# One decoder layer on one core: when the weight splits around the first stick-breaking head are queued

## The chip, the cores and the metric

The kernel runs on one core of one Trainium2 chip. The metric is the device time of one execution in microseconds. The kernel before took 1089.22 us, the median of three runs (1088.9 to 1090.16). A change of less than about 0.2% (2.2 us) can hardly be told from no change here.

The engines are named as the profile names them: PE (TensorE, matrix products), PEld (its weight loads), DVE (VectorE), ACT (ScalarE), POOL (GpSimd) and SP (SyncE, whose queue issues most loads).

## What is computed

One layer of a decoder on 512 tokens of width 1024, all in fp32. A combined projection of the input gives queries, keys and values for three kinds of attention, and gates. The branch that matters here is stick-breaking attention, eight heads of 64 columns:

```python
z = jnp.einsum('bhqd,bhkd->bhqk', qi, kt).astype(jnp.float32) * scale
log_keep = jnp.where(before, jax.nn.log_sigmoid(-z), 0.0)
later = lax.cumsum(log_keep, axis=3, reverse=True) - log_keep
a = jnp.where(before, jnp.exp(jax.nn.log_sigmoid(z) + later), 0.0)
return jnp.einsum('bhqk,bhkd->bhqd', a.astype(vt.dtype), vt)
```

The other two branches (differential and dilated attention) follow in time, then the output projection, a layer norm, an MLP and a second layer norm. None of these is touched.

## The kernel before, in words

**Products in fp32 precision.** Every fp32 operand is written as a high part (rounded to the matrix format) and a low part (the rest), and a product is three matmuls: high by high, high by low, low by high. A weight block of 128x1024 arrives from DRAM as `raw`; the *split* of a block is one ACT cast (`wh<-raw`, L227) and one DVE subtraction (`wl<-raw,wh`, L228). It is issued by `split_next` through `issue_split`.

**Items and blocks.** The work is a list of items, in the order of the main loop (L1326). An item is a group of 24 matmuls into one PSUM bank, and its evacuation (`ev`) is issued at the start of the next turn of the loop. The items and weight blocks that matter here are these:

| turn n | item | blocks it needs |
|---|---|---|
| 0 | queries and keys of the first pair of heads (`sb_q 0`, `sb_k 0`), two banks | 0 to 12 (input and first weights) |
| 1, 2 | `sb_q 1`, `sb_k 1` | 13; 14 |
| 3 to 6 | the first 512-column group: values `sb_v`, four row tiles | 15 to 18, all four for each tile |
| 7 to 10 | `sb_q 2`, `sb_k 2`, `sb_q 3`, `sb_k 3` | 19; 20; 21; 22 |

The items use two PSUM banks (tag `mm`) in turn: item 3 needs the bank of item 1 evacuated, item 4 that of item 2. Item 1 is evacuated by `evac_twice` (ACT L125, L126, L129, L131; DVE L108 twice, L130, L132) and item 2 by `evac_stacked` (ACT L115, L116; DVE L108 twice).

**How far ahead blocks are split.** `pump(limit, most)` issues at most `most` splits, and no further than `limit + 7` blocks, for seven pairs of `wh`/`wl` buffers; `fill` issues the loads, four `raw` buffers deep, so that the load of a block follows the split of the block four before. Up to the loop, blocks 0 to 13 are split. Then one block is split in turn 0 and one in turn 1 (blocks 14 and 15), two in turn 2 (16, 17), two in turn 3 (18, 19), and one each in turns 4 and 5 (20, 21). The limit stops turn 6; block 22 follows in turn 7.

**The heads.** `step` (L1302) advances the attention heads, which are generators, in between. Head 0 starts in the middle of turn 1: its score matmuls (L138, L139, masks L1004 and L1007) and then its softplus in three parts, `bi` = 2, 1, 0. A part is Abs, Exp, Ln on ACT (L1015 to L1017), then max-and-add, cast and subtraction on DVE (L1018, L1021, L1022). Part 2 is issued in turn 1, part 1 in turn 2, part 0 in turn 3. Triangle matmuls (L1048, L1052) use the results.

**What sets the order on each engine.** Each engine works through its queue in order, but the queue is not the source order. A planner fills it: source order is the priority, and an instruction further down goes first when the planner reckons that the earlier one cannot start yet. In the trace of before, the cast of block 15 sits between L131 and L115 though the source has it behind both. `tc.issue_after(x)` forces what is issued inside it to stand behind `x` on `x`'s own engine. The list `tie` is used for that: head 0's part 2 puts its Ln (ACT) and its subtraction L1022 (DVE) into it, and `issue_split` then keeps the splits of turns 2 to 4 (blocks 16 to 20) behind them; `tie` is emptied in turn 4.

Of the kernel before, what the change touches and what calls it, by code (L numbers as in the profile page):

```python
# [12 lines left out]
AF = mybir.ActivationFunctionType  # L13
# [42 lines left out]
def trunk(tc, a, out):  # L56
    nc = tc.nc
    es = ExitStack()
    with es:
# [85 lines left out]
        st = {"dma": 0, "sum": 0, "split": 0}  # L145
# [61 lines left out]
        tie = []  # L207
# [7 lines left out]
        def split_next():  # L215
            c = chunks[st["split"]]
            w = c["w"]
            if c.get("dst") is None:
                h = ring.tile([P, 1024], F32R, name=nm("wh"), tag="wh", bufs=RING)
                lo = ring.tile([P, 1024], F32R, name=nm("wl"), tag="wl", bufs=RING)  # L220
                parts = [(h[:, :w], lo[:, :w], 0, w)]
                c["h"], c["l"] = parts[0][:2]
            else:
                parts = c["dst"]
            for h, lo, a0, a1 in parts:
                raw = c["from"]["raw"][:, a0:a1]
                nc.scalar.copy(h, raw)  # L227
                i = nc.vector.tensor_sub(lo, raw, h.bitcast(F32))  # L228
                st["low"] = getattr(i, "ins", i)
            c["from"]["uses"] -= 1  # L230
            st["split"] += 1
# [760 lines left out]
        def sb_head(hd):  # L992
            pr, side = hd // 2, hd % 2
            rs = (A, B)[side]
            while ("sb_q", pr) not in T or ("sb_k", pr) not in T:
                yield
            blk = [(0, 0, 0, 512), (1, 1, 0, 384), (2, 2, 0, 256), (3, 2, 256, 256)]
            bank = [at_bank() for _ in range(3)]
            for kb, bi, c0, n in reversed(blk):
                ps = bank[bi][:, c0:c0 + n]  # L1000
                mm_pair(ps, T["sb_k", pr], T["sb_q", pr], side, slice(kb * P, kb * P + P), slice(S - n, S),
                        kb != 2, False)
                if kb == 3:
                    nc.tensor.matmul(ps, identb, mask_b.rearrange("p a b -> p (a b)"), start=False, stop=False,  # L1004
                                     skip_group_check=True)
                else:
                    nc.tensor.matmul(ps[:, 0:P], identb, mask_b[:, 1, :], start=False, stop=False,  # L1007
                                     skip_group_check=True)
            w = [512, 384, 512]
            sph, spl, later = {}, {}, {}  # L1010
            for bi in (2, 1, 0):
                n = w[bi]
                ps = bank[bi][:, :n]
                e = slot("e")[:, :n]
                nc.scalar.activation(e, ps, AF.Abs)  # L1015
                nc.scalar.activation(e, e, AF.Exp, scale=-1.0)
                ln = nc.scalar.activation(e, e, AF.Ln, bias=1.0)  # L1017
                nc.vector.scalar_tensor_tensor(e, ps, 0.0, e, op0=OP.max, op1=OP.add)  # L1018
                h = slot("sph", F32R)[:, :n]
                lo = slot("spl", F32R)[:, :n]  # L1020
                nc.vector.tensor_copy(h, e)  # L1021
                low = nc.vector.tensor_sub(lo, e, h.bitcast(F32))  # L1022
                if hd == 0 and bi == 2:

                    tie[:] = [getattr(i, "ins", i) for i in (ln, low)]
                sph[bi], spl[bi] = h, lo

                if bi == 2:
                    later[2] = (256, (h[:, HC], lo[:, HC]))
                    sm = slot("sm")[:, HB]  # L1030
                    nc.vector.tensor_add(sm, e[:, HB], e[:, HC])
                    hl = slot("smp", F32R)
                    nc.vector.tensor_copy(hl[:, HB], sm)
                    nc.vector.tensor_sub(hl[:, HC], sm, hl[:, HB].bitcast(F32))
                    later[1] = (256, (hl[:, HB], hl[:, HC]))
                elif bi == 1:
                    nc.vector.tensor_add(e[:, 128:384], e[:, 128:384], sm)
                    h = slot("smh", F32R)[:, :n]
                    lo = slot("sml", F32R)[:, :n]
                    nc.vector.tensor_copy(h, e)  # L1040
                    nc.vector.tensor_sub(lo, e, h.bitcast(F32))
                    later[0] = (384, (h, lo))
                yield
            ah, al = {}, {}
            for kb, bi, c0, n in reversed(blk):
                ps = bank[bi][:, c0:c0 + n]
                for hl in (sph, spl):
                    nc.tensor.matmul(ps, tri_r, hl[bi][:, c0:c0 + n], start=False, stop=False, skip_group_check=True)  # L1048
                if kb < 3:
                    n2, hl = later[kb]  # L1050
                    for t in hl:
                        nc.tensor.matmul(bank[bi][:, c0 + n - n2:c0 + n], ones_r, t, start=False, stop=False,  # L1052
                                         skip_group_check=True)
                if kb == 3:
                    continue
                n = w[bi]
                e = slot("a")[:, :n]
                nc.scalar.activation(e, bank[bi][:, :n], AF.Exp)
                h = slot("ah", F32R)[:, :n]
                lo = slot("al", F32R)[:, :n]  # L1060
                nc.vector.tensor_copy(h, e)
                nc.vector.tensor_sub(lo, e, h.bitcast(F32))
                ah[bi], al[bi] = h, lo
                if kb != 1:
                    yield
            while ("sb_v", 0, 3) not in V:
                yield
            po = at_bank()
            for kb, bi, c0, n in blk:
                v = V["sb_v", 0, kb][hd // 4][:, hd % 4]  # L1070
                nc.tensor.matmul(po[:, S - n:S], v.rearrange("p two d -> p (two d)"), ah[bi][:, c0:c0 + n],
                                 start=kb == 0, stop=False, skip_group_check=True)
                nc.tensor.matmul(po[A, S - n:S], v[:, 0, :], al[bi][:, c0:c0 + n], start=False, stop=kb == 3,
                                 skip_group_check=True)
            done = 4 + pr in oT
            if not done:
                oT[4 + pr] = slot("oT")
            t = slot("ot")
            nc.scalar.copy(t[A], po[B, :])
            nc.vector.tensor_add(oT[4 + pr][rs, :], po[A, :], t[A])  # L1080
            if done:
                split_sb(pr)
            yield
# [240 lines left out]
        freed = 8  # L1324
        prev = None
        for n, it in enumerate(items):  # L1326
            if n == first_branch[0]:
                while any(4 + k not in oTs for k in range(8)):
                    step()
            if n == first_da[0]:  # L1330
                while active or waiting:
                    step()
            need = it["need"] or it["c"]
            while any("h" not in c for c in need):
                pump(freed, 1)
            if prev is not None:
                prev[0]["ev"](prev[1])

            pump(freed, 1 if n < 10 and n != 2 else 2)
            if n == 4:  # L1340
                tie.clear()
                with tc.issue_after(st["load"]):
                    load_consts()
            if n == 10:
                with tc.issue_after(st["low"]):
                    make_lam()
            if n == 13:
                pending.append(tables())
            if n == 22:
                turn_tables()  # L1350
            if n == DA_TABS:
                da_tables()
            if n == DA_TABS + 4:
                turn_da()
            if n == wout_at - 9:
                load_pT()
            if n == wout_at - 1:
                ln_consts("ln1_g", "ln1_b")
                for tt in range(4):
                    load_xn(tt)  # L1360
            if n == wout_at + 24:
                ln_consts("ln2_g", "ln2_b")
            if n > 1:
                step()
            ps = it["bank"]() if it["bank"] else mm_bank()
            for _ in it["mm"](ps) or ():
                if HALF:
                    step()
            freed += len(it["c"])
            pump(freed, 0 if n < 10 else 2)  # L1370
            prev = (it, ps)
            if n + 1 < len(items) and n >= wout_at and pending:
                pass
# [99 lines left out]
```

## Time and profile before

| | |
|---|---|
| median of three runs | 1089.22 us |
| profiled execution | 1088.82 us, span 1087.1 us |
| PE busy | 1074.0 us, 99% of the span |
| DVE busy | 691.8 us, 64% |
| ACT busy | 477.6 us, 44% |
| mean granted TensorE clock | 0.996 |

A row of the timeline gives start (us), duration (us), engine, line, operation, output and input, shape, count, and in square brackets the idle time of the engine before it with what ended it. A matmul row lasts longer than the step to the next one, since matmuls overlap: the pace is read from the starts. A row of the table by windows gives the stretch, its length, and for each engine its busy time and instructions, then the granted clock (1.00 is full), the busy share of the DMA engines and GB/s.

### The profile page before, as it was taken

Reading aid. Unit: us, or ns where it says so; the run is one execution under the profiler, and the core shown is the slowest. Engines: PE = TensorE matmul, PEld = TensorE weight load, DVE = VectorE, ACT = ScalarE, POOL = GpSimd, SP = SyncE. Lnnn points to the kernel's source line nnn. Section 1 sums busy time; section 2 is a strip of 40 time slices with the busy share of each in tenths; the row PEclk is TensorE's granted clock in tenths of the full one; section 3 lists DMA queues with packets and bytes.
Section 4 is the critical chain, followed back from the end, with each engine's and each line's share of the span. In section 5 each row is a group of like instructions: output and inputs, shape, how many; then the busy total and the mean of one; then the engine's idle time right before and its main releaser. Section 6 shows DMA issues by size and latency. Waiting matters only on the chain.

```text
span 1087.1 us, 13105 instructions
## 1 busy us (share of the span) xinstructions
PE 1074.0 (99%) x4991; PEld 894.2 (82%) x4991; DVE 691.8 (64%) x1245; ACT 477.6 (44%) x795; POOL 31.3 (3%) x55
## 2 busy tenths in 40 slices
PE   9899999999999999999999999999999999999997
PEld 6788788999888888888888888888888888888886
DVE  5788577657453757655444463866686686686676
ACT  6665445335232545454333232323554454454441
POOL 0000200000000000000000020110000000000000
PEclk9999999999999999999999999999999999999998
DMA  7432412031322113222233352253222422322402
GB/s 251 128 108 75 117 59 94 24 116 63 112 78 78 60 38 107 68 78 87 90 99 103 98 203 97 82 180 103 82 97 80 134 97 79 135 96 79 135 1 78
DMA packets 32431, 105.71 MB, mean 97 GB/s; under 512 B 4378, under 2 KB 5290, under 8 KB 32368
## 3 DMA queue, kind: packets, MB, share of 16 engines
q1 hardware_dynamic: 29424, 96.91, 27.4%
q0 software_dynamic: 2368, 7.05, 2.0%
q8 instruction: 39, 0.64, 0.2%
q10 hardware_dynamic: 576, 0.92, 0.2%
q14 instruction: 24, 0.20, 0.1%
HBM read 102.74 MB, written 2.12 MB: 96 GB/s over the span
## 4 chain that ended last, share of the span: by engine, by line
PE 94%; DVE 3%; DMA 1%; ACT 1%; issue 1%; DVEq 0%; SPq 0%
PE mm L87 17%; PE mm L89 17%; PE mm L88 17%; PE mm L337 3%; PE mm L339 3%; PE mm L338 3%; PE mm L679 2%; PE mm L681 2%; PE mm L680 2%; PE at L679 2%; PE at L681 2%; PE at L680 2%; PE mm L510 1%; PE mm L574 1%; PE mm L575 1%; PE mm L509 1%
## 5 line engine op out<-in xcount | busy, mean ns | idle before, releaser
L227 ACT CAST wh<-raw 128x1024 fp32r<-128x1024 f32 (+1 forms) x173 | 178.2, 1032 | 290.1 <-PE mm L88 222.8
L228 DVE TENSOR_TENSOR wl<-raw,wh 128x1024 fp32r<-128x1024 f32 (+1 forms) x173 | 206.1, 1196 | 104.6 <-ACT wh L227 100.6
L87 PE MATMUL mm<-xhT,wh 128*128 128x512 f32 x496 | 196.5, 396 | 0.0
L89 PE MATMUL mm<-xhT,wl 128*128 128x512 f32 x496 | 194.2, 391 | 0.1
L88 PE MATMUL mm<-xlT,wh 128*128 128x512 f32 x496 | 193.8, 391 | 0.0
L89 PEld LDWEIGHTS mm<-xhT,wl 128*128 128x128 f32 x496 | 93.1, 188 | 20.2 <-DVE wl L228 0.5
L87 PEld LDWEIGHTS mm<-xhT,wh 128*128 128x128 f32 x496 | 93.3, 188 | 19.5 <-issue 1.1
L88 PEld LDWEIGHTS mm<-xlT,wh 128*128 128x128 f32 x496 | 93.3, 188 | 17.8
L88 PE MATMUL mm<-x1lT,wh 128*128 128x512 f32 x256 | 99.6, 389 | 0.0
L89 PE MATMUL mm<-x1hT,wl 128*128 128x512 f32 x256 | 99.6, 389 | 0.0
L87 PE MATMUL mm<-x1hT,wh 128*128 128x512 f32 x256 | 99.6, 389 | 0.0
L337 PE MATMUL mm<-wh,xhT 128*128 128x512 f32 x160 | 65.5, 409 | 2.4 <-DVE sb_kb L108 2.3
L339 PE MATMUL mm<-wh,xlT 128*128 128x512 f32 x160 | 63.6, 398 | 0.0
L338 PE MATMUL mm<-wl,xhT 128*128 128x512 f32 x160 | 63.6, 397 | 0.0
L89 PEld LDWEIGHTS mm<-x1hT,wl 128*128 128x128 f32 x256 | 48.1, 188 | 10.1
L88 PEld LDWEIGHTS mm<-x1lT,wh 128*128 128x128 f32 x256 | 48.1, 188 | 10.0
L87 PEld LDWEIGHTS mm<-x1hT,wh 128*128 128x128 f32 x256 | 48.0, 188 | 9.9
L227 ACT CAST wh<-wsum 128x1024 fp32r<-128x1024 f32 x28 | 29.5, 1055 | 52.5 <-PE mm L88 49.3
L228 DVE TENSOR_TENSOR wl<-wsum,wh 128x1024 fp32r<-128x1024 f32 x28 | 34.2, 1222 | 24.2 <-ACT wh L227 23.6
L337 PEld LDWEIGHTS mm<-wh,xhT 128*128 128x128 f32 x160 | 38.2, 239 | 6.4 <-issue 2.7
L339 PEld LDWEIGHTS mm<-wh,xlT 128*128 128x128 f32 x160 | 38.3, 239 | 4.0
L338 PEld LDWEIGHTS mm<-wl,xhT 128*128 128x128 f32 x160 | 38.5, 241 | 3.5
(348 smaller groups left out, 1969.1 us busy)
## 6 DMA issues: line engine op xcount, KB each, us to landing
raw<-in_wt_dram SPq DMA_DIRECT2D x62, 512.0 KB, 3.4
raw<-in_wu_dram SPq DMA_DIRECT2D x32, 512.0 KB, 3.4
raw<-in_wd_dram SPq DMA_DIRECT2D x32, 512.0 KB, 3.3
raw<-in_wv_dram SPq DMA_DIRECT2D x20, 512.0 KB, 3.4
raw<-in_wb_dram SPq DMA_DIRECT2D x8, 512.0 KB, 3.3
raw<-in_wo_dram SPq DMA_DIRECT2D x8, 512.0 KB, 4.0
raw<-in_wg_dram SPq DMA_DIRECT2D x8, 512.0 KB, 3.9
rawx<-in_xT_dram SPq DMA_DIRECT2D x8, 256.0 KB, 5.1
```

Source lines behind the costliest of these rows:

```text
L87: nc.tensor.matmul(ps, wh, xh, start=start, stop=False, skip_group_check=True)
L88: nc.tensor.matmul(ps, wh, xl, start=False, stop=False, skip_group_check=True)
L89: nc.tensor.matmul(ps, wl, xh, start=False, stop=stop, skip_group_check=True)
L227: nc.scalar.copy(h, raw)
L228: i = nc.vector.tensor_sub(lo, raw, h.bitcast(F32))
L337: nc.tensor.matmul(ps, x1, c["h"][:, s], start=k == 0, stop=False)
L338: nc.tensor.matmul(ps, x1, c["l"][:, s], start=False, stop=False)
L339: nc.tensor.matmul(ps, x2, c["h"][:, s], start=False, stop=k == 7)
L509: nc.tensor.matmul(ps, h[:, q], c["l"][:, s], start=False, stop=False)
L679: nc.tensor.matmul(ps, h[:, q], c["h"][:, s], start=go, stop=False, skip_group_check=True)
L680: nc.tensor.matmul(ps, h[:, q], c["l"][:, s], start=False, stop=False, skip_group_check=True)
L681: nc.tensor.matmul(ps, lo[:, q], c["h"][:, s], start=False, stop=end, skip_group_check=True)
```

## The change

Three things are edited, all in the order of issue; no computation is added or removed.

1. The number of splits per turn: turn 1 issues three (blocks 15, 16, 17) where it issued one, turn 2 one (18) where it issued two, and turns 3 and 4 none where they issued two and one. Turns 5 to 9 then issue blocks 19 to 23, one each. The source comes back to the old count at turn 11.
2. Blocks 16 and 17 are issued ahead of head 0's first softplus part and are not tied. Instead that part's Abs is forced to stand behind the last cast issued so far on ACT, which is that of block 17.
3. Every softplus part of head 0 now rewrites `tie`, and `tie` is emptied in turn 8. So block 18 (turn 2) is tied behind part 2, and blocks 19 to 22 (turns 5 to 8) are tied behind part 0's Ln on ACT and its subtraction on DVE. Block 23 (turn 9) is not tied.

The small constants (`load_consts`) are still issued in turn 4 behind the last load issued by then.

```diff
@@ split_next
-                nc.scalar.copy(h, raw)
+                i = nc.scalar.copy(h, raw)
+                st["cast"] = getattr(i, "ins", i)
@@ sb_head
-                nc.scalar.activation(e, ps, AF.Abs)
+                with ExitStack() as behind:
+                    if hd == 0 and bi == 2:
+
+                        behind.enter_context(tc.issue_after(st["cast"]))
+                    nc.scalar.activation(e, ps, AF.Abs)
...
-                if hd == 0 and bi == 2:
+                if hd == 0:
 
                     tie[:] = [getattr(i, "ins", i) for i in (ln, low)]
@@ main loop
-            pump(freed, 1 if n < 10 and n != 2 else 2)
+            pump(freed, {1: 3, 3: 0, 4: 0}.get(n, 1 if n < 10 else 2))
+            if n == 8:
+                tie.clear()
             if n == 4:
-                tie.clear()
                 with tc.issue_after(st["load"]):
                     load_consts()
```

## The prediction

> **What bounds the kernel now.** The list of what PE waited for comes first, since PE is busy 99% of the span. Columns: who waited, for whom, us in total, times, the longest.
>
> ```profile
> PE mm L337 <- DVE sb_kb L108: 2.3, 1, 2.3
> PE at L845 <- DVE rel L881: 1.3, 1, 1.3
> PE at L1048 <- DVE spl L1022: 0.9, 1, 0.9
> PE at L318 <- ACT wh L227: 0.4, 1, 0.4
> ```
>
> These four are all the waits of matmuls in the whole run. The second and fourth belong to the start. The other two are one place, and the table by windows shows what follows them:
>
> ```profile
> 40.00:44.00 4.00, 0.98 (x4) 0.81 (x5) 3.84 (x8) 0.86 (x2) 0.00 (x0) 0.97 0.90 259
> 44.00:48.00 4.00, 4.00 (x12) 3.11 (x12) 3.26 (x7) 0.87 (x2) 0.00 (x0) 0.60 0.41 139
> 48.00:54.00 6.00, 6.00 (x28) 4.95 (x27) 0.85 (x2) 2.43 (x6) 0.00 (x0) 1.00 0.00 0
> ```
>
> Between 40 and 44 us PE is busy for 0.98 us and DVE for 3.84: for these few us DVE is the bound. After it PE is busy again, but at a granted clock of 0.60. The timeline of PE gives the size of the loss:
>
> ```profile
> 35.18 0.39 PE L339 MATMUL mm<-wh,xlT 128*128 128x512 f32 x1
> ...
> 39.26 0.40 PE L339 MATMUL mm<-wh,xlT 128*128 128x512 f32 x1
> 39.50 0.33 PE L1048 MATMUL at<-sph,tri_r 128*128 128x384 f32 x1
> 40.74 0.44 PE L1048 MATMUL at<-spl,tri_r 128*128 128x384 f32 x1 [0.92 <-DVE spl L1022]
> 41.02 0.39 PE L1052 MATMUL at<-smp,ones_r 128*128 128x256 f32 x2
> 43.69 0.71 PE L337 MATMUL mm<-wh,xhT 128*128 128x512 f32 x1 [2.27 <-DVE sb_kb L108]
> ...
> 47.18 0.40 PE L339 MATMUL mm<-wh,xlT 128*128 128x512 f32 x1
> 47.41 0.40 PE L337 MATMUL mm<-wh,xhT 128*128 128x512 f32 x1
> ...
> 62.54 0.39 PE L87 MATMUL mm<-xhT,wh 128*128 128x512 f32 x1
> ...
> 75.70 0.34 PE L1048 MATMUL at<-sph,tri_r 128*128 128x384 f32 x1
> ...
> 76.29 0.40 PE L1048 MATMUL at<-sph,tri_r 128*128 128x512 f32 x1
> ```
>
> From 35.18 to 39.26 PE does 18 steps, 0.227 us each. From 39.50 to 47.41 it does two L1048, two L1052 and nine item matmuls (8 at half pace, for 43.69 to 47.18 is 3.49 us where 8 x 0.227 = 1.81 would do). Undisturbed, the first four take 76.29 - 75.70 = 0.59 us (the same four for head 1, between the last two rows) and the nine 2.04, together 2.63. The stretch took 7.91, so **5.3 us** are lost here: 0.92 + 2.27 of waiting, 1.7 by the clock, and 0.4 in hand-overs. That is 0.48% of the time, and the most that this region can give back. As no matmul waits later, what is gained here reaches the end.
>
> Why DVE is late, from its timeline (first rows of the region to the release of PE):
>
> ```profile
> 24.50 0.69 DVE L108 SCALAR_TENSOR_TENSOR sb_kb<-at,sb_kb 64x512 fp32r<-64x512 f32 x1
> 27.46 0.69 DVE L1018 SCALAR_TENSOR_TENSOR e<-at,e 128x512 f32<-128x512 f32 x1 [2.26 <-ACT e L1017]
> 28.18 0.43 DVE L1021 CAST sph<-e 128x512 fp32r<-128x512 f32 x1
> 28.64 0.69 DVE L1022 TENSOR_TENSOR spl<-e,sph 128x512 fp32r<-128x512 f32 x1
> ...
> 29.59 1.22 DVE L228 TENSOR_TENSOR wl<-raw,wh 128x1024 fp32r<-128x1024 f32 x1
> ...
> 30.93 1.22 DVE L228 TENSOR_TENSOR wl<-raw,wh 128x1024 fp32r<-128x1024 f32 x1
> ...
> 33.10 0.69 DVE L108 SCALAR_TENSOR_TENSOR sb_qlb<-mm,sb_qb 64x512 fp32r<-64x512 f32 x1
> ...
> 34.74 2.36 DVE L228 TENSOR_TENSOR wl<-raw,wh 128x1024 fp32r<-128x1024 f32 x2
> ...
> 37.60 1.21 DVE L228 TENSOR_TENSOR wl<-raw,wh 128x1024 fp32r<-128x1024 f32 x1
> ...
> 39.00 1.22 DVE L228 TENSOR_TENSOR wl<-raw,wh 128x1024 fp32r<-128x1024 f32 x1
> ...
> 42.85 0.69 DVE L108 SCALAR_TENSOR_TENSOR sb_kb<-mm,sb_kb 64x512 fp32r<-64x512 f32 x1
> ...
> 46.23 0.42 DVE L350 TENSOR_TENSOR sb_v<-mm,sb_v 128x256 fp32r<-128x256 f32 x1 [0.44 <-ACT sb_v L349]
> ```
>
> DVE idles 2.26 us at 25.2, then works without a pause until item 2's keys are evacuated at 43.54. The six subtractions in between are blocks 16 to 21, of which 19 to 21 are for items 7 to 9; item 7's first matmul is the L87 row at 62.54.
>
> **The change, part by part.**
>
> *Blocks 16 and 17 ahead of the first softplus.* Two casts and two subtractions move, no instruction is added. On ACT they meet this:
>
> ```profile
> 20.84 1.05 ACT L227 CAST wh<-raw 128x1024 fp32r<-128x1024 f32 x1
> 21.92 0.59 ACT L115 ACTIVATE sb_ka<-at 64x512 fp32r<-64x512 f32 x1
> 22.52 0.59 ACT L116 ACTIVATE sb_kb<-at 64x512 fp32r<-64x512 f32 x1
> 25.50 0.60 ACT L1015 ACTIVATE e<-at 128x512 f32<-128x512 f32 x1 [2.38 <-PE at L1007]
> ...
> 36.50 1.06 ACT L227 CAST wh<-raw 128x1024 fp32r<-128x1024 f32 x1 [0.59 <-DMA raw<-in_wt_dram]
> 37.46 0.59 ACT L115 ACTIVATE sb_ka<-mm 64x512 fp32r<-64x512 f32 x1
> ```
>
> The casts take 2 x 1.05 = 2.10 of ACT's 2.38 idle us (23.1 to 25.2), so Abs still starts at 25.5: cost 0, covered by the wait for the score matmuls; without that cover it is 2.1. On DVE the subtractions take 2 x 1.22 = 2.44 from 25.19, so L1018 starts at 27.63 and not 27.46: 0.17 us. Their old places fall free, 2.44 us ahead of 43.54.
>
> *The wait of Abs behind the cast of block 17.* Behind the cast stand Abs and all of the softplus, whose DVE steps and L1048 wait for it. It costs something only if block 17's data come late. The loads of that group issued after 18 us (durations of the issue in ns) and all landing times from 18 to 24 us are these:
>
> ```profile
> DMA to landing us min/median/max: 3.4/3.4/4.2
> L185 SPq DMA_DIRECT2D raw<-in_wv_dram x2: 328/328/328, 18.6 to 20.3; - x2
> ```
>
> Block 17 is the first: 18.6 + 4.2 = 22.8 at the latest, ahead of 24.15 where its cast would start. Bounds 0 and 0.6 (ACT's wait for a load at 36.50); I take 0, since the load is in by 1.3 us. On SP load 19 still follows the split of 15; loads 20 and 21 follow 16 and 17, whose subtractions end near 26.4 and 27.6 and not at 30.8 and 32.2, so they come some 4 us earlier. Load 23 follows split 19 and comes later, for a block of item 11. The seven small constants now stand in SP's queue behind load 22 and ahead of 23; their readers come at turn 10 and after. Cost 0.
>
> *Blocks 19 to 21 behind part 0.* Three subtractions, 3.66 us, and three casts leave the stretch ahead of 43.54. Their new cover is behind part 0: in the 48 to 54 row DVE idles for 5.15 of 6 us and ACT for 3.57, room for four subtractions (4.88) and three casts (3.15), ahead of item 7, which on the new time scale starts at 62.54 - 5.3 = 57.2. On DVE the rows up to the L350 at 46.23 leave no room before. Without that cover each late block costs PE its lateness. Bounds: 0, and 5.3 if the first one is done only when item 7 starts in before; I take 0, since the idle row is next to part 0's end. Head 1's softplus, which shares these engines, can be put off by at most the same three splits, and its triangle matmuls with it; PE has items 5 and 6 to do meanwhile.
>
> *Blocks 22 and 23.* 22 waits for the buffer pair that item 6 frees, before and after. 23 is issued in turn 9 and not 8, two items ahead of its use: 2 x 24 x 0.227 = 10.9 us of matmuls cover a split of 2.3. Cost 0; without the cover 2.3.
>
> *The sum.* DVE would reach 43.54 + 0.17 - 2.44 - 3.66 = 37.6 with item 2's evacuation. If part 0's three DVE steps (0.69 + 0.43 + 0.69 = 1.81) come forward into the space, 39.4. ACT permits it: 37.46, where L115 stands, loses casts 16, 17, 20, 21 and the wait, 4 x 1.05 + 0.59 = 4.8 us. PE, freed of the 0.92 as L1022 is earlier by the same 6 us, asks for the bank at 39.50 + 0.59 = 40.1. Next late is item 3's evacuation for item 5, asked for at 40.1 + 24 x 0.227 = 45.5. It ended at 46.23 + 0.42 = 46.65, and with 16 and 17 gone from in front of it at 44.4 even if 19 to 21 stay there. So both waits go, and with them the half clock: -5.3. I give back 0.3 for hand-overs: -5.0. From the profiled 1088.82 (span 1087.1 + 1.72 around it) that gives 1083.8; the median is 0.4 above the profiled run, so **1084.2**.
>
> **The clock rule.** Here 2.27 us of waiting, 0.92 before, and 0.4 to 0.98 us of work between led to 3.5 us at half pace. The Trainium skill, "TensorE: Matmul & The Clock Gate", section "What's actually happening", states that the clock falls after an idle window of some 3.4 us and comes back after a busy one, the windows running free. The length of the slow stretch agrees (3.49); the wait that led to it is shorter than the rule's, 2.27, or 3.19 with both. By the rule a leftover wait of 1 or 2 us would cost no clock (a leftover of 2 gives -3.3), by the row it may cost 1.7 again (-1.6).
>
> **Rivals.**
>
> *A. The wait moves to the other bank.* Item 3 needs item 1's evacuation, and PE now fills the time until then with head 1's scores:
>
> ```profile
> 31.92 0.28 PE L138 MATMUL at<-sb_qb,sb_kb 128*128 128x256 f32 x1
> ```
>
> The evacuation ends with the L108 at 33.10, at 33.8. If the planner puts item 3 ahead of these scores, PE stands from 31.9. One of the two subtractions ahead of that L108 goes, so it ends at 33.8 - 1.22 + 0.17 = 32.7: wait 0.8; at 33.8 if other work fills in: 1.9. With or without 1.7 of clock the gain is 1.7 to 4.5, 1084.7 to 1087.5, middle 1086.1. For it: DVE is full there. Against: the planner's order avoids this wait now.
>
> *B. The casts go ahead of the first keys.* Block 15's cast stands ahead of L115 (20.84), so 16 and 17 could too. Then sb_ka waits 2 x 1.22 = 2.4 us more on DVE, the scores with it; PE waits up to 2.4, plus 1.7 of clock, while DVE's idle time comes back. The old waits still go, for 3.66 us leave DVE and 3.2 are needed. Gain 1.2 to 5.3; I put it at 1086.3 to 1088.0, the half of full price, since item 2 could fill the wait.
>
> *C. It does nothing.* Part 0 and the head's sums take all the space freed on DVE, and item 2's keys stay late: 1089.2. From 37.6 it takes 2.5 us of other work ahead of L108 before PE waits at all and 5.9 to restore the old wait; part 0 has 1.81. Hardly.
>
> *D. Slower: a starved item 7.* Split 19 now stands behind part 0 and has the lowest priority of what is in the queue by then. This is where the subtraction of block 25 stands now:
>
> ```profile
> 64.32 1.21 DVE L228 TENSOR_TENSOR wl<-raw,wh 128x1024 fp32r<-128x1024 f32 x1
> ```
>
> If the planner puts block 19's there, it ends at 65.5; PE waits 65.5 - 57.2 = 8.3 us, plus 1.7 of clock: -5.3 + 10.0 = +4.7, 1093.9. It decides from an end at 63 on (57.2 + 5.8, with 5.8 + 1.7 - 5.3 = 2.2). Against it: the idle engines from 48 to 54, and no other reader of these engines that is more urgent there.
>
> **How the numbers follow.** Forecast 0.50, A 0.17, B 0.13, C 0.06, D 0.14 (with whatever else the new order delays). Forecast and A are faster by over 0.2% (under 1087.0; that bound is about what a measurement tells from no change), and half of B: 0.735. Within it lie the other half of B and C: 0.125. Slower: D. Forecast, A and B hold 0.80, so the range reaches from 1083.3 (the full 5.3 and 0.6 of scatter, as the runs before have) to 1088.0, B's end. The likeliest case alone: 1083.3 to 1085.4 (a rest of 1.2 us).
>
> **What would show it.** Right: two subtractions between sb_kb and L1018 in DVE's timeline with no idle 2.26; Abs still near 25.5; at most one subtraction of a block between L1022 of part 2 and sb_kb of item 2; no row of PE with sb_kb or spl as releaser; granted clock 1.00 from 40 to 48; item 7's first L87 near 57. Wrong: a wait of PE at its scores (B), on sb_qlb (A), or on wl at items 7 to 10 (D); or any wait after 62 us, which would mean that the planner's order changed further down.

## The result, and the profile after

The changed kernel takes 1082.47 us (median of five runs, 1082.22 to 1083.37) against 1089.22 us of the kernel before (five runs, the three named above and two more, 1087.84 to 1090.16). The ratio is 0.994, with a 95% interval from 0.9926 to 0.9955. The profiled execution took 1082.86 us with a span of 1081.2, that is 5.9 us of span less than before. The prediction had the direction, the place and the mechanism; its time of 1084.2 was 1.7 us too high, and the measured time lies 0.8 us below the range.

The list of what matmuls waited for, in the changed kernel (lines behind the edit have moved down by one to five: L1022 of before is L1027 here, L228 is L229, L337 is L338):

```profile
PE at L846 <- DVE rel L882: 1.3, 1, 1.3
PE at L319 <- ACT wh L227: 0.7, 1, 0.7
PE at L1123 <- DVE lg L1118: 0.2, 1, 0.2
```

Both waits of the region, on `sb_kb` and on `spl`, are gone. What is left is the start and 0.2 us far down. The table by windows, same columns as before:

```profile
40.00:44.00 4.00, 4.00 (x19) 3.34 (x18) 4.00 (x6) 1.16 (x3) 0.00 (x0) 1.00 0.50 156
44.00:48.00 4.00, 4.00 (x20) 3.36 (x20) 1.91 (x5) 2.66 (x6) 0.00 (x0) 1.00 0.70 269
48.00:54.00 6.00, 6.00 (x29) 4.98 (x28) 4.65 (x11) 2.15 (x4) 0.00 (x0) 1.00 0.02 5
```

PE is busy all the time and the granted clock stays at 1.00. DVE still has full windows, but nobody waits for it. Its timeline shows where the block subtractions (L229) went:

```profile
24.51 2.36 DVE L229 TENSOR_TENSOR wl<-raw,wh 128x1024 fp32r<-128x1024 f32 x2
27.20 0.69 DVE L1023 SCALAR_TENSOR_TENSOR e<-at,e 128x512 f32<-128x512 f32 x1 [0.33 <-ACT e L1022]
...
29.33 1.22 DVE L229 TENSOR_TENSOR wl<-raw,wh 128x1024 fp32r<-128x1024 f32 x1
...
31.84 0.69 DVE L108 SCALAR_TENSOR_TENSOR sb_qlb<-mm,sb_qb 64x512 fp32r<-64x512 f32 x1
...
37.18 0.69 DVE L108 SCALAR_TENSOR_TENSOR sb_kb<-mm,sb_kb 64x512 fp32r<-64x512 f32 x1
...
39.70 1.22 DVE L229 TENSOR_TENSOR wl<-raw,wh 128x1024 fp32r<-128x1024 f32 x1
...
41.17 1.21 DVE L229 TENSOR_TENSOR wl<-raw,wh 128x1024 fp32r<-128x1024 f32 x1
...
42.64 1.21 DVE L229 TENSOR_TENSOR wl<-raw,wh 128x1024 fp32r<-128x1024 f32 x1
```

Blocks 16 and 17 fill the idle time in front of the softplus (0.33 us of 2.26 is left), block 18 stands alone behind part 2, and 19 to 21 come behind part 0. Item 2's keys are evacuated at 37.87 us where it was 43.54. On ACT the two casts fit as well:

```profile
22.91 2.00 ACT L227 CAST wh<-raw 128x1024 fp32r<-128x1024 f32 x2
25.24 0.60 ACT L1020 ACTIVATE e<-at 128x512 f32<-128x512 f32 x1 [0.33 <-PE at L1008]
```

Abs still waits for the score matmuls (L1008), not for a cast. On PE, items 3, 4 and 7 now start here:

```profile
33.08 0.40 PE L139 MATMUL at<-sb_qlb,sb_kb 128*128 128x512 f32 x1
33.31 0.39 PE L338 MATMUL mm<-wh,xhT 128*128 128x512 f32 x1
...
39.06 0.40 PE L338 MATMUL mm<-wh,xhT 128*128 128x512 f32 x1
...
58.31 0.47 PE L87 MATMUL mm<-xhT,wh 128*128 128x512 f32 x1
```

The same moments in the kernel before:

```profile
33.58 0.23 PE L1007 MATMUL at<-mask_b,identb 128*128 128x128 bf16 x1
33.95 0.47 PE L337 MATMUL mm<-wh,xhT 128*128 128x512 f32 x1
```

and 43.69 for item 4, 62.54 for item 7. Counting item matmuls from the start of both traces, the 13th of item 1 starts at 20.98 before and 20.97 after. From there the changed kernel gains 0.26 us by the middle of item 2 and 0.38 by the start of item 3 (33.95 to 33.31, together 0.64), another 3.99 by the start of item 4 and 1.67 by item 4's 13th matmul, and gives back 0.42 for triangle matmuls that now run behind item 4 instead of ahead of it: 5.9, which stays to the end.

### The profile page after: what moved, and what is told of

Its sections match the earlier page's. It is cut to its first block, busy times and chain, and to the rows that moved or that the text cites. A ratio compares the mean times of both kernels' runs of the same rounds, so it can differ in the third digit from the quotient of the medians.

```text
span 1081.2 us, 13107 instructions
## 1 busy us (share of the span) xinstructions
PE 1071.2 (99%) x4991; PEld 893.2 (83%) x4991; DVE 691.6 (64%) x1245; ACT 478.2 (44%) x795; POOL 31.3 (3%) x55
## 4 chain that ended last, share of the span: by engine, by line
PE 96%; DVE 2%; DMA 0%; ACT 0%; issue 0%; SPq 0%; DVEq 0%
PE mm L87 18%; PE mm L88 18%; PE mm L89 18%; PE mm L338 3%; PE mm L340 3%; PE mm L339 3%; PE mm L682 2%; PE mm L681 2%; PE mm L680 2%; PE at L682 2%; PE at L681 2%; PE at L680 2%; PE mm L577 1%; PE mm L575 1%; PE mm L509 1%; PE mm L510 1%
## 5 line engine op out<-in xcount | busy, mean ns | idle before, releaser
L229 DVE TENSOR_TENSOR wl<-raw,wh 128x1024 fp32r<-128x1024 f32 (+1 forms) x173 | 206.1, 1197 | 103.8 <-ACT wh L227 99.9
L338 PE MATMUL mm<-wh,xhT 128*128 128x512 f32 x160 | 64.6, 404 | 0.0
L229 DVE TENSOR_TENSOR wl<-wsum,wh 128x1024 fp32r<-128x1024 f32 x28 | 34.2, 1222 | 24.2 <-ACT wh L227 23.6
L338 PEld LDWEIGHTS mm<-wh,xhT 128*128 128x128 f32 x160 | 37.9, 237 | 3.5
```

Of the source, the lines that this page charges most:

```text
L338: nc.tensor.matmul(ps, x1, c["h"][:, s], start=k == 0, stop=False)
```

## The experiments

The first four kernels ran beside one another, and so did the last three, each group with runs of the kernel before beside it (medians 1088.52 of ten and 1088.5 of thirteen). The start of a run varies with the arrival of the first loads (shown under the fourth experiment), so the table also gives the span from the 13th matmul of item 1 to the end; on that scale the kernel before has 1066.1 and the changed one 1060.2. Of this 5.9, 0.25 is not the change's (see the step that failed, below); it stands in every difference to before on this scale. The last two columns are those of the profiled execution of each kernel.

| kernel | median us | ratio to before (95%) | span | from item 1's 13th matmul | wait on `sb_kb` | clock |
|---|---|---|---|---|---|---|
| early pair alone | 1084.94 | 0.9967 (0.9955 to 0.9979) | 1083.3 | 1062.1 | 1.32 | holds |
| deferral alone | 1083.51 | 0.9955 (0.9938 to 0.9972) | 1081.9 | 1061.0 | 0.30 | holds |
| tie left at part 2 | 1084.5 | 0.9967 (0.9954 to 0.998) | 1082.7 | 1062.0 | 1.31 | holds |
| without the rule for Abs | 1082.53 | 0.9947 (0.9932 to 0.9962) | 1080.5 | 1060.2 | none | holds |
| block 16 early alone | 1086.99 | 0.9985 (0.9975 to 0.9994) | 1086.1 | 1064.9 | 2.26 | falls |
| deferral by two more turns | 1082.94 | 0.9952 (0.9937 to 0.9967) | 1081.4 | 1060.3 | none | holds |
| block 18 early too | 1083.03 | 0.9954 (0.9937 to 0.9972) | 1081.2 | 1060.1 | none | holds |

**The early pair alone.** Against the changed kernel:

```diff
-                if hd == 0:
+                if hd == 0 and bi == 2:
...
-            pump(freed, {1: 3, 3: 0, 4: 0}.get(n, 1 if n < 10 else 2))
-            if n == 8:
-                tie.clear()
+            pump(freed, {1: 3, 2: 0}.get(n, 1 if n < 10 else 2))
             if n == 4:
+                tie.clear()
```

> Blocks 16 and 17 are split ahead of the first softplus as in the changed kernel, but blocks 18 to 21 keep their old turns and are tied to part 2 only. Theory 1 (what counts is how many block subtractions stand in DVE's queue ahead of item 2's evacuation, L108 sb_kb): three more subtractions than in the changed kernel, 3 x 1.22 = 3.7 us, put the end of sb_kb at 37.9 + 3.7 = 41.5 us; PE asks at about 39.3 to 39.9, so it waits 1.6 to 2.2 us. Span 1082.8 to 1083.4 if the clock holds, 1084.5 to 1085.1 if it falls to half for one more stretch of 3.4 us. Rival (the idle time of DVE in front of the first softplus was the whole matter): no wait, span 1081.2.

The row of PE, and the subtractions and the evacuation on DVE:

```profile
41.49 0.47 PE L338 MATMUL mm<-wh,xhT 128*128 128x512 f32 x1 [1.32 <-DVE sb_kb L108]
```

```profile
24.72 2.36 DVE L229 TENSOR_TENSOR wl<-raw,wh 128x1024 fp32r<-128x1024 f32 x2
...
29.54 1.22 DVE L229 TENSOR_TENSOR wl<-raw,wh 128x1024 fp32r<-128x1024 f32 x1
30.88 1.22 DVE L229 TENSOR_TENSOR wl<-raw,wh 128x1024 fp32r<-128x1024 f32 x1
...
34.69 1.23 DVE L229 TENSOR_TENSOR wl<-raw,wh 128x1024 fp32r<-128x1024 f32 x1
36.42 1.22 DVE L229 TENSOR_TENSOR wl<-raw,wh 128x1024 fp32r<-128x1024 f32 x1
...
40.65 0.69 DVE L108 SCALAR_TENSOR_TENSOR sb_kb<-mm,sb_kb 64x512 fp32r<-64x512 f32 x1
```

Four block subtractions stand ahead of the evacuation behind the softplus, where the changed kernel has one. `sb_kb` ends at 41.34, near the 41.5 of theory 1, and PE waits 1.32 us, somewhat less than the 1.6 to 2.2 expected because the triangle matmuls fill part of it. The clock holds. The rival falls: DVE's idle time was not the whole matter. The pair alone is worth 4.0 us of 5.9. Item 3 starts 0.37 us after the last mask product here (33.53 to 33.90), as in the kernel before (33.58 to 33.95):

```profile
33.53 0.23 PE L1008 MATMUL at<-mask_b,identb 128*128 128x128 bf16 x1
33.90 0.47 PE L338 MATMUL mm<-wh,xhT 128*128 128x512 f32 x1
```

**The deferral alone.** Against the changed kernel:

```diff
-                with ExitStack() as behind:
-                    if hd == 0 and bi == 2:
-
-                        behind.enter_context(tc.issue_after(st["cast"]))
-                    nc.scalar.activation(e, ps, AF.Abs)
+                nc.scalar.activation(e, ps, AF.Abs)
...
-            pump(freed, {1: 3, 3: 0, 4: 0}.get(n, 1 if n < 10 else 2))
+            pump(freed, {2: 3, 3: 0, 4: 0}.get(n, 1 if n < 10 else 2))
```

> Blocks 19 to 21 wait for part 0 as in the changed kernel, but blocks 16, 17 and 18 are all issued in turn 2, tied behind part 2. Theory 1: DVE's idle 2.3 us in front of L1018 comes back (0.33 is left of it in the changed kernel), so sb_kb ends near 37.9 + 1.9 = 39.8 and PE waits 0.7 at most; item 3 starts later by about 0.5, as before. Span 1081.7 to 1082.4, clock full. Rival (the early pair carries the gain): the wait of some 2 us on sb_kb stays and the clock falls, span 1085 or more.

DVE, and PE at item 4 (the softplus lines stand one below those of before here, so L1018 of the text above is L1019):

```profile
27.12 0.69 DVE L1019 SCALAR_TENSOR_TENSOR e<-at,e 128x512 f32<-128x512 f32 x1 [2.72 <-ACT e L1018]
...
39.36 0.69 DVE L108 SCALAR_TENSOR_TENSOR sb_kb<-mm,sb_kb 64x512 fp32r<-64x512 f32 x1
```

```profile
40.20 0.47 PE L338 MATMUL mm<-wh,xhT 128*128 128x512 f32 x1 [0.30 <-DVE sb_kb L108]
```

The idle time is back (2.72 us), the evacuation ends at 40.05, and PE waits 0.30 us. Theory 1 had 39.8 and at most 0.7. The deferral alone is worth 5.1 us of 5.9. The two gains do not add: 4.0 + 5.1 is more than there was to lose. Both parts work on the same wait, of which the pair alone leaves 1.32 us and the deferral alone 0.30, and with either the granted clock stays at 1.00 here.

**The tie left at part 2.** One line against the changed kernel:

```diff
-                if hd == 0:
+                if hd == 0 and bi == 2:
```

> The changed kernel with one thing undone: the tie stays at part 2 of the softplus and is not moved on to parts 1 and 0, while the splits are issued in the new turns. Theory 1: the planner puts blocks 19 to 21 into DVE's queue ahead of sb_kb again, so this goes like the early pair alone: wait 1.6 to 2.2 us, span 1082.8 to 1085.1. Rival (the new turns alone hold the splits back, the moved tie is idle): span 1081.2, no wait.

The last two of the four block subtractions that stand behind the softplus and ahead of item 2's evacuation, and PE:

```profile
34.18 1.23 DVE L229 TENSOR_TENSOR wl<-raw,wh 128x1024 fp32r<-128x1024 f32 x1
...
35.91 1.22 DVE L229 TENSOR_TENSOR wl<-raw,wh 128x1024 fp32r<-128x1024 f32 x1
...
40.15 0.69 DVE L108 SCALAR_TENSOR_TENSOR sb_kb<-mm,sb_kb 64x512 fp32r<-64x512 f32 x1
```

```profile
40.99 0.47 PE L338 MATMUL mm<-wh,xhT 128*128 128x512 f32 x1 [1.31 <-DVE sb_kb L108]
```

PE waits 1.31 us on `sb_kb` again, and from item 1 on the run is 1062.0 us long, the early pair alone 1062.1. So it is the moved tie that holds blocks 19 to 21 back; issuing them some turns later in the source does not, since the planner fills DVE with them as soon as they are allowed. The rival falls. The opposite, the moved tie with the old turns, was not run; there block 19 would be tied behind part 1 and not part 0.

**Without the rule for Abs.** The five lines around Abs are taken out as in the deferral alone, and nothing else.

> The changed kernel without the rule that Abs of part 2 stands behind the cast of block 17. Theory 1: the early pair already comes first in the source, and the planner has the data in time, so nothing changes: span 1081.2, within 0.2. Rival (the pin is what puts the pair in front): the pair goes behind the softplus and the span is that of the deferral alone, 1081.7 to 1082.4. If it is the same program in effect, its times beside the changed kernel's also show the scatter of one program.

The queues of all five engines come out the same as in the changed kernel, instruction by instruction. The rule for Abs does nothing in this order. The run is then a second look at one program, and shows its scatter. The second cast of the input waits for its load on ACT, first in this run and then in the changed kernel's:

```profile
5.98 0.62 ACT L227 CAST xhT<-rawx 128x512 fp32r<-128x512 f32 x1 [1.01 <-DMA rawx<-in_xT_dram]
```

```profile
6.64 0.62 ACT L227 CAST xhT<-rawx 128x512 fp32r<-128x512 f32 x1 [1.60 <-DMA rawx<-in_xT_dram]
```

The 13th matmul of item 1 starts at 20.27 here and at 20.97 there, 0.70 us apart, and so are the spans (1080.5 and 1081.2). Behind item 1 the two runs are equal to 0.1 us.

**Block 16 early alone.** As the early pair alone, with `{1: 2}` as the only exception in the number of splits per turn.

> As the early pair alone, but only block 16 goes ahead of the first softplus; 17 and on stay as in the kernel before. It asks how long a wait must be before the clock falls. Theory 1 (DVE's queue): sb_kb of item 2 ends one subtraction later than with the early pair alone, which had PE wait 1.3 us: a wait of 2.4 to 2.6 us. If the clock holds: span 1084.4 to 1084.9. If a wait of that length costs a stretch at half clock: 1086.1 to 1086.6. A clock that falls only after some 3.4 us with almost no matmul says the first.

PE around item 4's start, and two windows of 3.4 us on either side of the moment at which the pace changes:

```profile
42.64 0.47 PE L338 MATMUL mm<-wh,xhT 128*128 128x512 f32 x1 [2.26 <-DVE sb_kb L108]
...
43.40 0.46 PE L338 MATMUL mm<-wh,xhT 128*128 128x512 f32 x1
43.65 0.63 PE L339 MATMUL mm<-wl,xhT 128*128 128x512 f32 x1
...
46.64 0.56 PE L340 MATMUL mm<-wh,xlT 128*128 128x512 f32 x1
47.04 0.40 PE L338 MATMUL mm<-wh,xhT 128*128 128x512 f32 x1
```

```profile
40.13:43.55 3.42, 1.16 (x7) 0.86 (x6) 3.29 (x6) 0.00 (x0) 0.00 (x0) 1.00 0.85 250
43.55:46.96 3.41, 3.41 (x10) 2.70 (x9) 2.70 (x6) 0.87 (x2) 0.00 (x0) 0.51 0.11 37
```

The wait is 2.26 us, a little under the 2.4 to 2.6 expected, and it is the only one in the region. The span, 1086.1, is the one expected if the clock falls, and the granted clock is 0.51 for 3.41 us. So in this execution one wait of this length cost another 1.7 us. PE runs at full pace from 42.64 and only from 43.65 at half, whereas in the kernel before it is at half pace from the first matmul on (43.69, the next at 44.20).

It is not the same in every execution of this kernel. Its ten spans fall into two groups: six from 1085.2 to 1086.4 us with a mean granted clock of 0.996, and four from 1083.7 to 1084.4 with 0.997 to 0.999. The 1.8 us between the groups' means are about the price of one slow stretch, so in the four the clock probably held; only the profiled execution, one of the six, has a trace. The kernel before has four such short spans among its 23 later runs (1084.8 to 1085.5; the others are 1086.2 to 1088.2). One run of block 18 early, further below, stands out in the same way (1082.8 at 0.996, its other three 1080.3 to 1081.4); it has no trace either, and the profiled execution of that kernel has no such wait.

**Deferral by two more turns.** The changed kernel with two entries more:

```diff
-            pump(freed, {1: 3, 3: 0, 4: 0}.get(n, 1 if n < 10 else 2))
+            pump(freed, {1: 3, 3: 0, 4: 0, 5: 0, 6: 0}.get(n, 1 if n < 10 else 2))
```

> The changed kernel with no split issued in turns 5 and 6 either: blocks 19 and 20 follow in turn 7, 21 in turn 8. Rival D of the prediction (splits behind part 0 come late for item 7) would show here first: a wait of PE on wl at item 7, span over 1083. Theory 1: the turn is only a priority; the planner fills DVE's gap behind part 0 with the same three subtractions near 40 to 44 us, 14 us ahead of item 7, and the span stays at 1080.5 to 1081.3.

```profile
39.79 1.22 DVE L229 TENSOR_TENSOR wl<-raw,wh 128x1024 fp32r<-128x1024 f32 x1
...
41.26 1.22 DVE L229 TENSOR_TENSOR wl<-raw,wh 128x1024 fp32r<-128x1024 f32 x1
...
42.73 1.22 DVE L229 TENSOR_TENSOR wl<-raw,wh 128x1024 fp32r<-128x1024 f32 x1
```

The same three subtractions stand 0.1 us from where the changed kernel has them, some 14 us ahead of item 7, and no wait comes up. The turn in the source only ranks the splits. Rival D of the prediction has no ground here.

**Block 18 early too.**

```diff
-            pump(freed, {1: 3, 3: 0, 4: 0}.get(n, 1 if n < 10 else 2))
+            pump(freed, {1: 4, 2: 0, 3: 0, 4: 0}.get(n, 1 if n < 10 else 2))
```

> The changed kernel with block 18 also split ahead of the first softplus, Abs behind its cast. Its load was issued at 20.3 us and lands by 24.5; its cast starts near 24.9 and ends at 25.9 where Abs started at 25.2. Theory 1: Abs and the softplus move back by 0.7 to 1.3 us, but the same subtraction leaves the place behind part 2, so sb_kb ends as early as before and no wait comes up: span 1080.5 to 1081.5. Rival (the softplus chain itself is what PE waits for, and the pair fits only because it is hidden): PE waits about 1 us at L1053 or L338, span 1082 or more.

DVE and ACT in front of the softplus:

```profile
24.61 3.50 DVE L229 TENSOR_TENSOR wl<-raw,wh 128x1024 fp32r<-128x1024 f32 x3
28.14 0.69 DVE L1023 SCALAR_TENSOR_TENSOR e<-at,e 128x512 f32<-128x512 f32 x1
```

```profile
25.98 0.60 ACT L1020 ACTIVATE e<-at 128x512 f32<-128x512 f32 x1
```

Abs starts at 25.98, 0.7 us later than in the changed kernel, and L1023 0.9 later. No matmul waits for it. The softplus itself has room; what PE needs in time is the evacuations behind it.

A version faster than the changed kernel did not come out of these runs, and this lever has next to nothing left: from the first items to the end the list of waits of the changed kernel has 0.2 us.

## Why the prediction was right in its mechanism, and where its size failed

**The waits.** Right. The whole of DVE's work ahead of item 2's evacuation was what PE waited for; with five of the six subtractions moved, `sb_kb` ends at 37.87, where the sum had 37.6. That this is so close is in part luck, as two errors nearly cancel. From the first softplus step on DVE to the end of `sb_kb` the time went from 16.08 to 10.67 us, so the five subtractions gave 5.41 us and not the 6.10 of the sum: a subtraction lasts 1.22, but the next step starts sooner than that (30.72 after 29.59). Against that, the softplus step starts at 27.20 and not at 27.63, since the evacuations ahead of the pair end 0.7 us earlier than in the trace of before (24.48 and 25.19). Part 0 did not come ahead of it but right behind. Both waits and the half clock went together: the stretch from item 3's start to item 4's regular pace, with the triangle matmuls that moved, gave 3.99 + 1.67 - 0.42 = 5.24 us, of 5.3 found in the trace of before.

**The early pair.** Right: the casts fit in front of Abs (25.24; 25.5 before), and the load of block 17 was in. The wait that the change puts on Abs cost nothing, for a stronger reason than the one given: the queue has the same order without it.

**The cover of blocks 19 to 21.** Right in the price, 0, and wrong in the place: they did not go into the window from 48 to 54, but directly behind part 0 (39.70 to 43.85), between the steps of item 3's evacuation.

**Rivals.** A and B did not come up: DVE kept sb_kb ahead of the pair, and PE kept head 1's scores ahead of item 3, but for their last mask product. C fell with the trace, and D with the trace and the run on later turns. Item 7 starts at 58.31 and not at 57.2, with value and triangle matmuls of head 0 and 1 ahead of it that ran later before; nothing waits there.

**The step that failed is the sum's "most that this region can give back", 5.3 us, of which 5.0 was kept.** The change itself gave 5.24 + 0.38 = 5.62 in the traces. The measured difference of the profiled runs is 1088.82 - 1082.86 = 5.96. Its terms: 5.24 where 5.0 was forecast, as the 0.3 held back for hand-overs were not lost. Then 0.38 at item 3's start, which stands ahead of the stretch that was measured. There PE started nothing between the last mask product at 33.58 and 33.95, waiting for item 1's evacuation (DVE L108, 33.10 to 33.79), which is below what the list of waits shows; the rows of rival A pass over it, since they treat that bank as covered by the scores. This 0.38 appears in every run with both parts and in none with only one of them, where a second subtraction still stands ahead of that evacuation (30.88 with the pair alone): it needs the pair and block 19 out of DVE's way. Another 0.26 between item 1 and the middle of item 2 is not the change's doing, as far as the runs tell: the deferral alone, which alters nothing that early on DVE, has the same 0.25. In the trace of before the cast of block 14 starts at 17.50 us behind its load, in that of the changed kernel at 16.52; DVE is 0.7 us later there, and PE's first scores wait a little for `sb_ka`. The remaining 0.1 is rounding and the time around the span.

The sum misses the profiled run by 1.0 of the 1.7 us. The rest, 0.8, is the step from the profiled run to the median. The forecast added 0.4 since the median of before lay above its profiled run; the changed kernel's median lies 0.4 below its own. With the later runs of before, whose medians are 1088.52 and 1088.5, and the twin's 1082.53, the gain by medians is 6.0 us and not 6.75, in line with the traces: so this part of the miss is the luck of the first runs and not a cost of the kernel. The lower end of the range, 1083.3, was the ceiling of 5.3 and 0.6 of scatter; it had neither the 0.38 nor so high a median of before in it.

**The clock rule.** The row was the better guide, not the page. The prediction left open whether a leftover wait of 2 us costs clock. It can: 2.26 us alone, in a window in which PE was busy for 1.16 of 3.42 us, brought half a clock in the profiled execution, though by the spans not in all ten; 1.32 us did not. The Trainium skill, "TensorE: Matmul & The Clock Gate", section "What's actually happening", speaks of an idle window of some 3.4 us. The length of the slow stretch agrees with it (3.41 us at 0.51); that the window must be idle does not, for a third of the 3.42 us ahead of the fall was busy, and with 2.26 us the longest wait there, no 3.4 us of that region is idle.

## What to carry to other kernels

When an engine that is idle on average makes the matmuls wait at one place, count what stands in its queue ahead of the instruction that is waited for, and sort that work by when it is needed: what has a free slot earlier goes there, what is needed later goes behind. Here each alone brought most of the gain (4.0 and 5.1 of 5.9 us), and the two do not add. A planner that fills idle time needs a tie to an instruction; moving the issue in the source without one, or by two turns more with it, changed nothing here.

Give the ceiling of such a gain from the first to the last hand-over that touches the engine, not only from the waits that a list shows: 0.38 us of standing still had no row of its own there.

## What the runs showed of the hardware that was not expected

The TensorE clock fell after a single wait of 2.26 us, in the profiled execution and, by the spans, in about six of ten, and held after one of 1.32. It then stayed at half for 3.41 us, though PE was busy all that time. That nearly doubles the price of such a wait: 2.26 us of waiting cost 1.7 more, as much as in the kernel before.

The fall did not follow the end of the wait. The waits of the two traces end at 43.69 (before) and 42.64 us (block 16 early alone), and the half pace begins with the first matmul behind it in the one and 1.0 us later in the other. By the clock records of both traces the fall comes 37.55 us after the clock's first rise, eleven times 3.41. A fixed beat of that length would also explain why some executions keep the clock, since a wait that is split between two beats weighs less in each; no run here shows that. In the 3.41 us ahead of the fall PE was busy for 0.74 us (before) and 1.15 us (block 16 early alone). With the tie left at part 2 the beat from 39.32 to 42.73 holds the whole wait of 1.31 us; PE was busy for 2.10 us of it, and the clock held. What lies in between was not tried.

One program varied by 0.7 us between two executions in its first 20 us alone, by when the first input blocks arrived; behind that, the two agree to 0.1 us.
